# Up projection of an encoder block: products gathered in two PSUM banks, the convolution summed in PSUM, and every engine's order written by hand

## The chip, the cores and the metric

One core of one Trainium2 chip. The metric is the device time of one execution in microseconds (us), lower is better. The kernel computes in float32 throughout.

## The reference

One layer of an encoder on 1024 tokens of width 1024: a norm, an input projection, a pooling mixer beside differential attention, an output projection with residual, then the part that matters here, the gated MLP (`D_FF` is 2816, so `w_up` is 1024 x 5632):

```python
h = rmsnorm(x, norm_ffn_g[l])
u = causal_dwconv(h @ w_up[l], conv_w[l], conv_b[l])      # out[t] = b + sum_j w[j] * u[t-2+j], per channel
gate, val = jnp.split(u, 2, axis=-1)
x = x + (jax.nn.silu(gate) * val) @ w_down[l]
return rmsnorm(x, norm_final_g)
```

## The kernel before, in words

**Products.** Float32 values are split into a rounded high part and a low rest (`split`, lines 83 to 91: ScalarE casts the high part on line 86, VectorE or GpSimd subtracts for the low part on line 87). One product of 128x128 weights with 512 columns is three matmuls (`mm3`, lines 78 to 81: high x high, high x low, low x high).

**Up projection.** The 5632 columns are taken as 22 blocks `f` (NF), each with 128 gate and 128 value channels. A block is a 2x2 by 2x2 block product: gate and value against the two halves of the contraction (weights a11, a12, a21, a22, each 128x512), and the two halves of the contraction against the two halves of the tokens (H = 512). It is done with seven products in place of eight: the sums S1 to S4 of the weights (GpSimd, lines 731 to 734) stand against sums T1 to T4 of the tokens' blocks, which `norm2b` makes once (lines 635 to 660). `product` (line 706) is 4 x 3 = 12 matmuls into one PSUM tile of 512 columns. So a block has 84 matmuls. Results, channels on the partitions and 1024 tokens along the free axis: `ug` (gate) and `uv` (value).

`up` (lines 739 to 782) issues per block P1 (operand B11), P6 (T2), P2 (B21), P5 (T1), P7 (T3), P4 (T4), P3 (B22). The sums of products are made by VectorE out of PSUM: on line 726 `ug` left = P2 + s1 (s1 is ScalarE's copy of P1, line 720), on line 748 u2 = P6 + s1, on line 758 u3 = P7 + u2, on line 759 u2 += P5, on line 760 `uv` right = P5 + u3, on line 765 `uv` left = u3 - P4, on line 767 `ug` right = P3 + u2. P6 and P7 lie in one PSUM tile of two banks, P5 and P3 in another (tag S, two tiles in all); P1, P2 and P4 take tiles of one bank (tag B, four).

**Convolution and gate.** For value and gate: ScalarE makes o = u * w + bias (line 773), VectorE adds two shifted taps (line 775, `scalar_tensor_tensor` of 1023 and 1022 columns, all of it in SBUF), ScalarE applies Silu to the gate (line 778), and GpSimd multiplies the two (line 780). `store` (lines 789 to 810) writes the result to DRAM as the operand of the down projection and makes sums of it on VectorE (line 797, or lines 803 to 805 for every second block).

**Ahead.** P1 and P2 of the first four blocks (AHEAD, lines 812 to 819) are computed while the last token blocks are normalized.

**What sets the order.** Outside of regions marked otherwise, the framework's scheduler orders each engine's instructions by a model of time and their place in the program. From line 825 on, where the down projection begins, the DMA queue (SP) is issued in program order. Down again has seven products, P1 to P7 of 11 x 4 x 3 matmuls (`load`, `unit`, lines 876 to 905), whose operands are read back, split and used three steps ahead.

**Buffers.** `raw` (4) holds loaded weights, `Q` (6) the sums S, `hi` and `lo` (5 each) split weights, `T` (5) s1, u2, u3, `K` (4) ug and uv, `E` (6) the tiles of the convolution.

Of the kernel before, what the change touches and what calls it, by code (L numbers as in the profile page):

```python
# [14 lines left out]
AF = mybir.ActivationFunctionType  # L15
# [4 lines left out]
T = 1024  # L20
# [30 lines left out]
def block_kernel(ctx, tc, x, xT, pos, wv, wqk, wp, wo, wup, wdn, cols, invf, rcnt, gffn, gfin,  # L51
# [25 lines left out]

    def mm3(dst, lhi, llo, rhi, rlo, first, last):
        mm(dst, lhi, rhi, start=first, stop=False)  # L79
        mm(dst, lhi, rlo, start=False, stop=False)  # L80
        mm(dst, llo, rhi, start=False, stop=last)  # L81

    def split(src, hi, lo, scale=None, eng=None):

# [550 lines left out]
    def norm2b(tt):  # L635
# [65 lines left out]

    acts, opd, ugs, s1s = {}, {}, {}, {}

    def product(dst, w, nm):
        hi, lo = opnd[nm]
        for kt in range(4):
            c = slice(kt * P, (kt + 1) * P)
            j, k = divmod(kt, 4 // len(hi))  # L710
            mm3(dst, w[0][:, c], w[1][:, c], hi[j][:, k, :], lo[j][:, k, :], kt == 0, kt == 3)

    add, sub = ALU.add, ALU.subtract
    tens = nc.vector.tensor_tensor

    def up_p1(f, w):
        p1 = psB(f"P1{f}")
        product(p1, w, "B11")
        s1s[f] = st("T", f"s1{f}")
        nc.scalar.copy(out=s1s[f], in_=p1)  # L720

    def up_p2(f, w):
        p2 = psB(f"P2{f}")
        product(p2, w, "B21")
        ugs[f] = st("K", f"ug{f}")
        tens(out=ugs[f][:, 0:H], in0=p2, in1=s1s[f], op=add)

    def up_prep(f, ahead):
        a11, a12, a21, a22 = [wraw(f, a, pc, "b" if ahead and a == 0 else "") for a in range(2) for pc in range(2)]
        S1, S2, S3, S4 = [st("Q", f"S{i}{f}") for i in range(4)]  # L730
        nc.gpsimd.tensor_tensor(out=S1, in0=a21, in1=a22, op=add)  # L731
        nc.gpsimd.tensor_tensor(out=S2, in0=S1, in1=a11, op=sub)  # L732
        nc.gpsimd.tensor_tensor(out=S3, in0=a11, in1=a21, op=sub)  # L733
        nc.gpsimd.tensor_tensor(out=S4, in0=a12, in1=S2, op=sub)  # L734
        return a11, a12, a22, S1, S2, S3, S4

    waiting = []

    def up(f, ahead, prep, then):
        a11, a12, a22, S1, S2, S3, S4 = prep  # L740
        if not ahead:
            up_p1(f, wsplit(a11, f"a11{f}"))
        s1 = s1s[f]
        p67 = psS(f"P67{f}")
        p6, p7 = p67[:, 0:H], p67[:, H:T]
        product(p6, wsplit(S2, f"S2{f}"), "T2")
        u2 = st("T", f"u2{f}")
        tens(out=u2, in0=p6, in1=s1, op=add)
        if not ahead:
            up_p2(f, wsplit(a12, f"a12{f}"))  # L750
        ug = ugs[f]
        uv = st("E" if f == order[0] else "K", f"uv{f}")
        p53 = psS(f"P53{f}")
        p5, p3 = p53[:, 0:H], p53[:, H:T]
        product(p5, wsplit(S1, f"S1{f}"), "T1")
        product(p7, wsplit(S3, f"S3{f}", nc.gpsimd), "T3")
        u3 = st("T", f"u3{f}")
        tens(out=u3, in0=p7, in1=u2, op=add)
        tens(out=u2, in0=p5, in1=u2, op=add)
        tens(out=uv[:, H:T], in0=p5, in1=u3, op=add)  # L760
        if waiting:
            store(*waiting.pop())
        p4 = psB(f"P4{f}")
        product(p4, wsplit(a22, f"a22{f}"), "T4")
        tens(out=uv[:, 0:H], in0=u3, in1=p4, op=sub)  # L765
        product(p3, wsplit(S4, f"S4{f}"), "B22")
        tens(out=ug[:, H:T], in0=p3, in1=u2, op=add)  # L767
        prep = then()
        acc = []
        for a, u in ((1, uv), (0, ug)):  # L770
            cc = 16 + (a * NF + f) * 4
            o = st("E", f"ac{f}{a}")
            nc.scalar.activation(o, u, AF.Identity, bias=col[:, cc + 3:cc + 4], scale=col[:, cc + 2:cc + 3])  # L773
            for d in (1, 2):
                nc.vector.scalar_tensor_tensor(out=o[:, d:T], in0=u[:, 0:T - d], scalar=col[:, cc + 2 - d:cc + 3 - d],  # L775
                                               in1=o[:, d:T], op0=ALU.mult, op1=ALU.add)
            if a == 0:
                nc.scalar.activation(o, o, AF.Silu)  # L778
            acc.append(o)
        nc.gpsimd.tensor_tensor(out=acc[1], in0=acc[1], in1=acc[0], op=ALU.mult)  # L780
        waiting.append((f, acc[1]))
        return prep
# [313 lines left out]
```

## Time and profile before

| | |
|---|---|
| median of 3 runs | 1082.02 us (1080.84 to 1086.27) |
| the profiled execution | 1083.04 us, of which the span of instructions is 1081.3 us |
| matmuls (PE) busy | 1022.4 us, 95% of the span |
| VectorE (DVE) busy | 883.2 us, 82% |
| ScalarE (ACT) busy | 484.1 us, 45% |
| GpSimd (POOL) busy | 417.6 us, 39% |
| mean granted TensorE clock | 0.991 of full speed |

The span runs from the first to the last instruction; the profiled execution's own time is 1.7 us longer. In rows of instructions the columns are start (us from the span's start), duration (us), engine, line of the kernel, operation, tile written <- tiles read, shapes, and in brackets how long the engine had been idle before it and what ended that. Matmuls overlap in the pipeline: a row of 0.39 us is followed by the next after 0.23 us, so the distance between starts is what one matmul costs. Tile names are cut by the profile: `P<-T,S16h` is a product of the up projection with the high part of S1 of block 6, `dP` one of the down projection.

### The profile page before, as it was taken

The page shows a single profiled execution, that of the slowest core. Times are in us where ns is not written, and L with a number is a line of the kernel's source. Part 1 is how long each engine was busy: PE and PEld are TensorE (multiplying, and loading weights), DVE is VectorE, ACT ScalarE, POOL GpSimd, SP SyncE. Part 2 cuts the span into 40 slices and gives each one's busy share as a digit, 9 for nine tenths or more (in the row PEclk, how much of TensorE's full clock was granted, in tenths as well). Part 3 has the DMA queues.
Part 4 walks back from the last instruction along what each step waited for, and adds up shares of the span by engine and source line. Part 5 has one row for each costly group of instructions (what it writes and reads, how often), then busy time and mean ns, then how long its engine had stood idle before and what let it go on. Part 6 is the DMA issues. An engine that isn't in the chain of part 4 may idle for free.

```text
span 1081.3 us, 13516 instructions
## 1 busy us (share of the span) xinstructions
PE 1022.4 (95%) x4612; PEld 834.9 (77%) x4612; DVE 883.2 (82%) x1195; ACT 484.1 (45%) x842; POOL 417.6 (39%) x306
## 2 busy tenths in 40 slices
PE   8999999998998998989999999999999899999995
PEld 6888888886886876767777778778778688877884
DVE  6465887989757496999988998898998976699895
ACT  6822554556546263333433333333334554334533
POOL 0000122221221066565465465465465100586462
PEclk9999999999999999999999999999999999999999
DMA  8627543323335222232222222222222885442215
GB/s 305 226 96 266 173 147 108 102 97 116 126 117 166 78 88 69 88 117 78 98 98 99 97 98 105 89 102 106 86 108 96 322 312 203 157 144 100 98 57 187
DMA packets 67972, 143.88 MB, mean 133 GB/s; under 512 B 8512, under 2 KB 9664, under 8 KB 67904
## 3 DMA queue, kind: packets, MB, share of 16 engines
q1 hardware_dynamic: 67904, 143.03, 37.7%
q8 instruction: 36, 0.59, 0.2%
q14 instruction: 32, 0.26, 0.1%
HBM read 105.78 MB, written 37.22 MB: 132 GB/s over the span
## 4 chain that ended last, share of the span: by engine, by line
PE 39%; DVE 16%; issue 14%; POOL 13%; DMA 3%; ACT 2%; POOLq 0%; SPq 0%; DVEq 0%; ACTq 0%
PE dP L80 5%; PE dP L81 5%; PE dP L79 5%; DVE ac L775 4%; POOL ac L780 3%; PE po L81 3%; PE po L79 2%; PE po L80 2%; PE sc L386 2%; POOL S L732 2%; PE O L433 2%; POOL S L734 2%; DMA wu<-in_wup 2%; POOL S L731 2%; PE P L79 2%
## 5 line engine op out<-in xcount | busy, mean ns | idle before, releaser
L403 POOL TENSOR_SCALAR e<-e,sm 128x128 f32<-128x128 f32 (+7 forms) x32 | 29.9, 936 | 175.6 <-DMA k<-tsk 69.5
L775 DVE SCALAR_TENSOR_TENSOR ac<-uv,col,ac 128x1023 f32<-128x1023 f32 (+1 forms) x44 | 78.2, 1777 | 6.3 <-ACT ac L773 5.7
L775 DVE SCALAR_TENSOR_TENSOR ac<-ug,col,ac 128x1023 f32<-128x1023 f32 (+1 forms) x44 | 76.6, 1741 | 0.8 <-ACT ac L773 0.7
L780 POOL TENSOR_TENSOR ac<-ac,ac 128x1024 f32<-128x1024 f32 x22 | 60.3, 2740 | 37.9 <-ACT ac L778 37.8
L731 POOL TENSOR_TENSOR S<-wu,wu 128x512 f32<-128x512 f32 x22 | 30.2, 1374 | 107.2 <-DMA wu<-in_wup 107.1
L773 ACT ACTIVATE ac<-uv,col 128x1024 f32<-128x1024 f32 x22 | 27.4, 1245 | 89.7 <-DVE uv L765 89.7
L399 ACT ACTIVATE e<-sc,mx 128x128 f32<-128x128 f32 (+7 forms) x64 | 47.2, 743 | 32.3 <-DVE mx L389 16.8
L773 ACT ACTIVATE ac<-ug,col 128x1024 f32<-128x1024 f32 x22 | 27.4, 1245 | 52.3 <-DVE ug L767 52.3
L386 PE MATMUL sc<-K,Q 128*128 128x512 f32 (+3 forms) x192 | 42.6, 351 | 0.7 <-ACT e L399 0.7
L853 POOL TENSOR_TENSOR T<-B22w,B12w 128x512 f32<-128x512 f32 x11 | 17.5, 1595 | 65.0 <-DMA arP<-S 63.3
L733 POOL TENSOR_TENSOR S<-wu,wu 128x512 f32<-128x512 f32 x18 | 37.4, 2079 | 0.0
L386 PEld LDWEIGHTS sc<-K,Q 128*128 128x128 f32 x192 | 32.4, 189 | 6.0 <-ACT e L399 1.2
L564 DVE TENSOR_TENSOR X<-X,po 128x512 f32<-128x512 f32 x32 | 21.6, 681 | 16.3 <-PE po L81 16.2
L421 ACT COPY at<-tp 128x512 f32<-128x512 f32 (+3 forms) x48 | 21.6, 484 | 28.8 <-PE tp L417 28.8
L778 ACT ACTIVATE ac<-ac 128x1024 f32<-128x1024 f32 x22 | 23.3, 1061 | 25.0 <-DVE ac L775 25.0
L433 PE MATMUL O<-at,V 128*128 128x256 f32 (+1 forms) x160 | 34.0, 358 | 0.0
L433 PEld LDWEIGHTS O<-at,V 128*128 128x128 f32 x160 | 29.8, 190 | 4.0
L389 DVE TENSOR_REDUCE mx<-sc 128x1 f32<-128x640 f32 (+3 forms) x32 | 32.2, 1014 | 0.4
L734 POOL TENSOR_TENSOR S<-wu,S 128x512 f32<-128x512 f32 x18 | 32.5, 1804 | 0.0
L732 POOL TENSOR_TENSOR S<-S,wu 128x512 f32<-128x512 f32 x18 | 31.3, 1738 | 1.4
L87 DVE TENSOR_TENSOR wP<-B12w,wP 128x512 fp32r<-128x512 f32 x30 | 26.4, 903 | 3.2 <-ACT wP L86 1.8
L404 DVE SCALAR_TENSOR_TENSOR e<-e,sm,e 128x640 f32<-128x640 f32 (+3 forms) x16 | 17.4, 1090 | 10.3 <-POOL e L403 10.3
(2488 smaller groups left out, 3645.4 us busy)
## 6 DMA issues: line engine op xcount, KB each, us to landing
wu<-in_wup SPq DMA_DIRECT2D x88, 256.0 KB, 2.6
S<-s SPq DMA_DIRECT2D x22, 512.0 KB, 3.2
arP<-S SPq DMA_DIRECT2D x44, 256.0 KB, 2.6
arP<-A SPq DMA_DIRECT2D x33, 256.0 KB, 4.3
Q<-q SPq DMA_DIRECT2D x64, 128.0 KB, 2.9
A<-ac SPq DMA_DIRECT2D x11, 512.0 KB, 2.9
xs<-in_x SPq DMA_DIRECT2D x8, 512.0 KB, 7.5
K<-k SPq DMA_DIRECT2D x8, 512.0 KB, 4.8
```

What stands on the lines that cost most here:

```text
L79: mm(dst, lhi, rhi, start=first, stop=False)
L80: mm(dst, lhi, rlo, start=False, stop=False)
L81: mm(dst, llo, rhi, start=False, stop=last)
L386: mm(sc[:, k0:k1], qst[h, grp][n * 2 + hl][:, qc], kst[h][n][:, k0:k1], start=hl == 0, stop=hl == 1)
L399: nc.scalar.activation(ee[n], scs[n][:, 0:L], AF.Exp, bias=nmx[:, n:n + 1], accum_out=sums[:, n:n + 1])
L433: mm(O[:, c0:256], V[j][:, h * P:(h + 1) * P], at[:, j, c0:256], start=j == 0, stop=j == nj - 1)
L731: nc.gpsimd.tensor_tensor(out=S1, in0=a21, in1=a22, op=add)
L732: nc.gpsimd.tensor_tensor(out=S2, in0=S1, in1=a11, op=sub)
L734: nc.gpsimd.tensor_tensor(out=S4, in0=a12, in1=S2, op=sub)
L773: nc.scalar.activation(o, u, AF.Identity, bias=col[:, cc + 3:cc + 4], scale=col[:, cc + 2:cc + 3])
L775: nc.vector.scalar_tensor_tensor(out=o[:, d:T], in0=u[:, 0:T - d], scalar=col[:, cc + 2 - d:cc + 3 - d], in1=o[:, d:T], op0=ALU.mult, op1= ...
L780: nc.gpsimd.tensor_tensor(out=acc[1], in0=acc[1], in1=acc[0], op=ALU.mult)
```

## The change

Only the up projection and its convolution are touched, and the place where they begin.

- P1, P6, P7 and P4 are added up by TensorE in one bank X, P5 and P3 in another, Z. ScalarE copies X out after each product but the first of them is s1: s1 after P1, u2 after P6, u3 after P7, `uv` left after P4. T4 changes its sign for this. VectorE keeps three sums: `ug` left = P2 + s1, `uv` right = Z + u3 (read between P5 and P3), `ug` right = Z + u2. The four ahead blocks keep separate banks for P6, P7, P4 and have VectorE add (five sums).
- ScalarE writes the convolution's o into PSUM (two-bank tiles, tag S), and VectorE's taps read and write it there. The gate's product moves from GpSimd to VectorE (`after4`).
- Weights are loaded two blocks ahead (`h`), a22 into a tile of tag Q; sums S are made one block ahead (`g`); the convolution of a block (`p`) runs beside the products of the next one.
- In the loop over blocks the order of all five queues is the order of the program. One block issues P6, P5, P7, P1 of the next, P4, P3, P2 of the next.

```diff
-    def mm3(dst, lhi, llo, rhi, rlo, first, last):
+    def mm3(dst, lhi, llo, rhi, rlo, first, last, more=False):
...
-        nc.gpsimd.tensor_tensor(out=t4, in0=t2, in1=t4, op=sub)
+        nc.gpsimd.tensor_tensor(out=t4, in0=t4, in1=t2, op=sub)
...
+    def conv(u, a, src):
+        cc = 16 + (a * NF + u.f) * 4
+        o = psS(f"o{a}{u.f}")
+        nc.scalar.activation(o, src, AF.Identity, bias=col[:, cc + 3:cc + 4], scale=col[:, cc + 2:cc + 3])
+        return o
+    def tap(u, a, d, src, o):
+        cc = 16 + (a * NF + u.f) * 4
+        nc.vector.scalar_tensor_tensor(out=o[:, d:T], in0=src[:, 0:T - d], scalar=col[:, cc + 2 - d:cc + 3 - d],
+                                       in1=o[:, d:T], op0=ALU.mult, op1=ALU.add)
...
+    def after0(p):
+        tap(p, 1, 1, p.uv, p.o1)
+        p.o0 = conv(p, 0, p.ug)
+    def after1(p):
+        tap(p, 1, 2, p.uv, p.o1)
+    def after2(p):
+        tap(p, 0, 1, p.ug, p.o0)
+    def after3(p):
+        tap(p, 0, 2, p.ug, p.o0)
+    def after4(p):
+        g = st("E", f"g{p.f}")
+        nc.scalar.activation(g, p.o0, AF.Silu)
+        p.act = st("E", f"ac{p.f}")
+        tens(out=p.act, in0=p.o1, in1=g, op=ALU.mult)
+    def up(p, u, g, h):
+        new = g is not None and not g.ahead
+        if u.ahead:
+            x6 = psB(f"P6{u.f}")
+        else:
+            x6 = u.X
+        product(x6, u.S2w, "T2", u.ahead)
+        up_split(u, "S3", nc.gpsimd)
+        if p:
+            after0(p)
+        if not u.ahead:
+            c11(u, u.Y)
+        if u.ahead:
+            u2 = u.s1
+            tens(out=u2, in0=x6, in1=u.s1, op=add)
+        else:
+            u2 = st("T", f"u2{u.f}")
+            nc.scalar.copy(out=u2, in_=x6)
+        z = psB(f"Z{u.f}")
+        product(z, u.S1w, "T1")
+        if new:
+            up_split(g, "a11")
+        if p:
+            after1(p)
+        if h:
+            up_load(h, "a21")
+        x7 = psB(f"P7{u.f}") if u.ahead else x6
+        product(x7, u.S3w, "T3", u.ahead)
+        up_split(u, "a22")
+        if p:
+            after2(p)
...
+            nc.scalar.copy(out=u3, in_=x7)
+        if new:
+            g.X = psB(f"P1{g.f}")
+            product(g.X, g.a11w, "B11")
+        up_split(u, "S4")
+        if p:
+            after3(p)
+        if g:
+            up_sum(g, 1)
+            up_sum(g, 3)
...
+        x4 = psB(f"P4{u.f}") if u.ahead else x6
+        product(x4, u.a22w, "T4", u.ahead)
+        u.uv = st("E" if u.n < 2 else "K", f"uv{u.f}")
+        tens(out=u.uv[:, H:T], in0=z, in1=u3, op=add)
+        if new:
+            g.s1 = st("T", f"s1{g.f}")
+            nc.scalar.copy(out=g.s1, in_=g.X)
+            up_split(g, "a12")
+        if p:
+            after4(p)
+        if g:
+            up_sum(g, 2)
...
+        product(z, u.S4w, "B22", False)
...
+            nc.scalar.copy(out=u.uv[:, 0:H], in_=x4)
+        if g:
+            up_split(g, "S2")
+        u.o1 = conv(u, 1, u.uv)
+        if p:
+            store_a(p)
+        if g:
+            up_sum(g, 4)
...
+        if new:
+            g.Y = psB(f"P2{g.f}")
+            product(g.Y, g.a12w, "B21")
+        if g:
+            up_split(g, "S1")
+        tens(out=u.ug[:, H:T], in0=z, in1=u2, op=add)
+        if p:
+            store_b(p)
...
+            up_load(u, "a21", "a22", "a11", "a12")
+            for k in (1, 3, 2, 4):
+                up_sum(u, k)
...
+    with tc.manual_schedule(engines={E.PE, E.Activation, E.DVE, E.Pool, E.SP}):
+        for n in range(NF):
+            up(us[n - 1] if n else None, us[n], us[n + 1] if n + 1 < NF else None, us[n + 2] if n + 2 < NF else None)
+        p = us[-1]
+        for fn in (after0, after1, after2, after3, after4, store_a, store_b):
+            fn(p)
```

`up_split` is the split of a weight tile (cast on ScalarE, rest on VectorE, for S3 on GpSimd), `up_sum` one of the sums S on GpSimd, `up_load` a load on SP, `c11` the sum on `ug`'s left half, `store_a` and `store_b` the two halves of the former `store`.

## Rows read from the trace of the kernel before

**Rows 1.** The page, parts 1 and 2: TensorE and VectorE busy, granted clock in 40 slices.

```profile
PE 1022.4 (95%) x4612; PEld 834.9 (77%) x4612; DVE 883.2 (82%) x1195; ACT 484.1 (45%) x842; POOL 417.6 (39%) x306
...
PEclk9999999999999999999999999999999999999999
```

**Rows 2.** Stretches, up's products only: stretch, length, PE busy (matmuls), clock, DMA share, GB/s.

```profile
388.30:418.50 30.20, 24.81 (x96) 0.94 0.26 88
418.50:517.95 99.45, 88.59 (x362) 0.97 0.27 98
517.95:820.24 302.29, 290.17 (x1260) 1.00 0.26 96
820.24:854.43 34.19, 30.23 (x130) 1.00 0.55 189
```

**Rows 3.** Timeline of TensorE: first and last of 22 matmuls without a wait.

```profile
843.56 0.39 PE L79 MATMUL P<-T,S321h 128*128 128x512 f32 x1
...
848.32 0.39 PE L81 MATMUL P<-T,a2221l 128*128 128x512 f32 x1
```

**Rows 4.** Waits of TensorE: who waited <- for whom: us in total, times, longest.

```profile
PE P L79 <- DVE ug L767: 15.7, 19, 1.7
...
PE P L79 <- DVE u L758: 4.6, 4, 3.2
```

**Rows 5.** Timeline, all engines, block 6: what stands before one of these waits.

```profile
654.47 0.39 PE L81 MATMUL P<-T,S26l 128*128 128x512 f32 x1
...
656.06 2.21 DVE L775 SCALAR_TENSOR_TENSOR ac<-uv,col,ac 128x1022 f32<-128x1022 f32 x1
...
658.19 0.68 DVE L767 TENSOR_TENSOR ug<-P,u 128x512 f32<-128x512 f32 x1
...
658.92 0.50 PE L79 MATMUL P<-T,S16h 128*128 128x512 f32 x1 [0.44 <-DVE ug L767]
```

**Rows 6.** The steady stretch: all engines, then VectorE's line 87 and its line 775.

```profile
517.95:820.24 302.29, 290.17 (x1260) 235.34 (x1260) 275.59 (x285) 115.95 (x166) 168.96 (x90) 1.00 0.26 96
...
517.95:820.24 302.29, 95.72 (x91) 1.00 0.26 96
...
517.95:820.24 302.29, 107.22 (x60) 1.00 0.26 96
```

**Rows 7.** VectorE by line: durations in ns, least/median/longest; out of PSUM, SBUF alone, into PSUM.

```profile
L759 DVE TENSOR_TENSOR u<-P,u x22: 676/678/680, 435.6 to 850.2; 128x512 f32<-128x512 f32 x22
...
L775 DVE SCALAR_TENSOR_TENSOR ac<-uv,col,ac x44: 1269/1490/2410, 439.9 to 857.0; 128x1023 f32<-128x1023 f32 x22, 128x1022 f32<-128x1022 f32 x22
...
L388 DVE MEMSET sc<- x32: 112/112/112, 124.4 to 306.0; 64x64 f32 x32
...
L392 DVE MEMSET sc<- x16: 165/165/165, 108.6 to 241.1; 64x128 f32 x16
```

**Rows 8.** ScalarE: the copy out of PSUM, the convolution's start, a cast.

```profile
L720 ACT COPY s<-P x22: 576/577/598, 399.0 to 836.2; 128x512 f32<-128x512 f32 x22
...
L773 ACT ACTIVATE ac<-uv,col x22: 1242/1245/1248, 437.5 to 853.3; 128x1024 f32<-128x1024 f32 x22
...
417.85 0.62 ACT L86 CAST S20h<-S 128x512 fp32r<-128x512 f32 x1 [0.50 <-POOL S L732]
```

**Rows 9.** GpSimd: the sum S2 of block 0, and the gate's product (line 780).

```profile
416.09 1.73 POOL L732 TENSOR_TENSOR S<-S,wu000b 128x512 f32<-128x512 f32 x1
...
L780 POOL TENSOR_TENSOR ac<-ac,ac x22: 2395/2842/2862, 454.6 to 864.3; 128x1024 f32<-128x1024 f32 x22
```

**Rows 10.** From TensorE to VectorE: a product's last matmul, and the reader that had waited.

```profile
438.90 0.39 PE L81 MATMUL P<-T,S211l 128*128 128x512 f32 x1
...
439.33 0.69 DVE L748 TENSOR_TENSOR u<-P,s 128x512 f32<-128x512 f32 x1 [1.84 <-PE P L81]
```

**Rows 11.** Timelines at the end of up: VectorE, and SP's last store of an activation.

```profile
844.16 0.68 DVE L87 TENSOR_TENSOR aP10l<-arP,aP10h 128x512 fp32r<-128x512 f32 x1
...
868.74 0.38 SPq L786 DMA_DIRECT2D A<-ac  x1
```

More of the change, by code (lines that the diff above doesn't have):

```diff
@@ L699, in block_kernel, with product @@
             norm2b(tt - 1)
-    acts, opd, ugs, s1s = {}, {}, {}, {}
-    def product(dst, w, nm):
+    acts, opd, U = {}, {}, {}
+    def product(dst, w, nm, first=True):
         hi, lo = opnd[nm]
@@ L710, in product @@
             j, k = divmod(kt, 4 // len(hi))
-            mm3(dst, w[0][:, c], w[1][:, c], hi[j][:, k, :], lo[j][:, k, :], kt == 0, kt == 3)
+            mm3(dst, w[0][:, c], w[1][:, c], hi[j][:, k, :], lo[j][:, k, :], first and kt == 0, kt == 3, not first)
     add, sub = ALU.add, ALU.subtract
     tens = nc.vector.tensor_tensor
[L716 to L782, printed above, removed]
@@ new lines, in block_kernel, with __init__, up_load, up_sum @@
+    pool = nc.gpsimd.tensor_tensor
+    class Up:
+        def __init__(u, n):
+            u.n, u.f, u.ahead = n, order[n], n < AHEAD
+    def up_load(u, *which):
+        for nm in which:
+            a, pc = {"a11": (0, 0), "a12": (0, 1), "a21": (1, 0), "a22": (1, 1)}[nm]
+            r = st("Q" if nm == "a22" else "raw", f"w{nm}{u.f}")
+            nc.sync.dma_start(out=r, in_=wup[u.f, a, :, pc * 4:pc * 4 + 4, :].rearrange("p a b -> p (a b)"))
+            setattr(u, nm, r)
+    def up_sum(u, k):
+        t = st("Q", f"S{k}{u.f}")
+        setattr(u, f"S{k}", t)
+        x, y, op = {1: ("a21", "a22", add), 2: ("S1", "a11", sub), 3: ("a11", "a21", sub), 4: ("a12", "S2", sub)}[k]
+        pool(out=t, in0=getattr(u, x), in1=getattr(u, y), op=op)
@@ L787, in dram, with store_a @@
         return t
-    def store(f, a):
-        i = f % NG
-        if f < NG:
+    def store_a(u):
+        i, a = u.f % NG, u.act
+        if u.f < NG:
             acts[i] = a
@@ L796, in store @@
             s34 = acts["s34"] = st("E", f"s34{i}")
-            nc.vector.tensor_tensor(out=s34[:, 0:H], in0=a[:, 0:H], in1=a[:, H:T], op=sub)
+            tens(out=s34[:, 0:H], in0=a[:, 0:H], in1=a[:, H:T], op=sub)
             return
@@ new lines, in up @@
+    def up(p, u, g, h):
[29 more added lines that the diff above has]
+            after2(p)
+        u3 = st("T", f"u3{u.f}")
+        if u.ahead:
+            tens(out=u3, in0=x7, in1=u2, op=add)
+        else:
+            nc.scalar.copy(out=u3, in_=x7)
[8 more added lines that the diff above has]
+            up_sum(g, 3)
+        if h:
+            up_load(h, "a22")
+        x4 = psB(f"P4{u.f}") if u.ahead else x6
[10 more added lines that the diff above has]
+            up_sum(g, 2)
+        if h:
+            up_load(h, "a11")
+        product(z, u.S4w, "B22", False)
+        if u.ahead:
+            tens(out=u.uv[:, 0:H], in0=u3, in1=x4, op=add)
+        else:
+            nc.scalar.copy(out=u.uv[:, 0:H], in_=x4)
[6 more added lines that the diff above has]
+            up_sum(g, 4)
+        if h:
+            up_load(h, "a12")
+        if new:
[6 more added lines that the diff above has]
+            store_b(p)
@@ L816, in block_kernel @@
+    us = [Up(n) for n in range(NF)]
+    for u in us[:AHEAD]:
+        x = psB(f"P1{u.f}")
+        product(x, ahead_w.pop(0), "B11")
+        u.s1 = st("T", f"s1{u.f}")
+        nc.scalar.copy(out=u.s1, in_=x)
+        y = psB(f"P2{u.f}")
+        product(y, ahead_w.pop(0), "B21")
+        c11(u, y)
+        if u.n == 0:
             norm2b(7)
-            first = up_prep(0, True)
+            up_load(u, "a21", "a22", "a11", "a12")
+            for k in (1, 3, 2, 4):
+                up_sum(u, k)
@@ L818, in block_kernel @@
             for tt in range(4, 8):
                 osplit("B22", tt, fb["B22", tt], nc.gpsimd if tt % 2 else None)
-    for n, f in enumerate(order):
-        first = up(f, n < AHEAD, first, lambda: up_prep(order[n + 1], n + 1 < AHEAD) if n + 1 < NF else None)
-    store(*waiting.pop())
+    up_split(us[0], "S2")
+    up_split(us[0], "S1")
+    up_load(us[1], "a21", "a22", "a11", "a12")
+    E = mybir.EngineType
+    with tc.manual_schedule(engines={E.PE, E.Activation, E.DVE, E.Pool, E.SP}):
[4 more added lines that the diff above has]
+            fn(p)
```

29 lines of the change are left out of this document (17 added, 12 removed).

## The prediction, made blind

> **What bounds the kernel now.** I read the page first: TensorE is busy 95% of the span, VectorE 82%, and the granted clock is at or near the upper level, 2.4 GHz, in all 40 slices [rows 1]. As rows of matmuls overlap, "95%" hides small gaps, so I then counted the up projection's matmuls in stretches [rows 2] and set against them what one costs without a wait: 22 in a row start 4.76 us apart from first to last, 4.76/21 = 0.2267 us each [rows 3]. A product is 12 of them, 2.72 us; a block 84, 19.04 us. Excess over that, by stretch:
>
> - 388.3 to 418.5 (the products ahead): 30.2 - 96 x 0.2267 = 8.4 us, some of it transposes of the norm.
> - 418.5 to 517.95 (the four ahead blocks and the way into the next): 99.45 - 362 x 0.2267 = 17.4 us.
> - 517.95 to 820.24 (15 steady blocks): 302.29 - 285.6 = 16.7 us, 1.11 per block; a block takes 20.15 us.
> - 820.24 to 854.43 (last block, into down): 34.19 - 29.5 = 4.7 us.
>
> After the first stretch that is 38.8 us, the most that this change can win. The waits of TensorE name the cause: 19 waits for line 767, `ug` right [rows 4]. One of them: P3 of block 6 issues its last matmul at 654.47, but VectorE is in the taps until 658.19 and only then reads the bank, which P5 of the next block needs; TensorE resumes at 658.92 [rows 5]. The bound of a steady block is VectorE being late, not the matmuls: it is busy 275.6 of 302.3 us [rows 6].
>
> **The change, engine by engine, per steady block.** TensorE: the same 84 matmuls, 19.04 us. The loads are as many as before (256 KB each) and DMA has room (share 0.26) [rows 2]; nothing for them. SP waits in order now: a load stands behind the store of `act`, but loads are two blocks ahead, 38 us, so that order hides.
>
> VectorE before: seven sums out of PSUM, six low parts, four taps, two sums of `store` on average; busy 275.6/15 = 18.4 us. Low parts cost 95.72/91 = 1.05 us, taps 107.22/60 = 1.79 us [rows 6]. A sum with a PSUM operand always takes 0.68, while a tap in SBUF takes 1.27 to 2.41 [rows 7]; what lengthens it is there only where both operands are in SBUF. After: three sums 2.04, six low parts 6.3, `store` 1.4, the gate's product about one tap, and four taps with o in PSUM. No row shows an instruction that reads and writes PSUM at once. Bounds: 1.27 us (the least tap; nothing suggests cheaper) to 2.54 (twice that, if reading and writing one bank took turns). The nearest rows: reading PSUM costs what SBUF does, and writing it costs (165 - 112)/64 = 0.83 ns per element [rows 7]. So I take 1.27; VectorE's sum is 2.04 + 6.3 + 1.4 + 5 x 1.27 = 16.1 us, under 19.04.
>
> ScalarE: 115.95/15 = 7.7 us [rows 6]; three more copies at 0.58 make 9.5 us, and writing o into PSUM is not shown; I leave it at 1.245 [rows 8] (twice that would be 2.5 more: 12 us, still no bound; less would free nothing that is waited for). GpSimd: 168.96/15 = 11.3 us [rows 6] less the gate's product, 2.84 [rows 9]: 8.4.
>
> Order decides the rest. In block time P6 ends at 2.72, P5 at 5.44, P7 at 8.16, P1 of the next at 10.88, P4 at 13.60, P3 at 16.32, P2 of the next at 19.04. A reader starts 0.43 us after the start of a product's last matmul [rows 10], so 0.2 after the next product's start. Three checks:
>
> - Handoffs in bank X: end of product, 0.2, copy 0.58, next product into X. About 0.85 us against the 2.72 of the other product between them. Queued on ScalarE behind such a copy are one or two casts of 0.6; before it, at most a cast and a convolution, 1.9 us. Covered.
> - Handoff in bank Z: VectorE must read P5 (with u3) before P3 at 13.60. Its order: `c11` 0.9; a11's low part waits for the cast behind u2's copy, 2.72 + 0.2 + 0.58 + 0.6 = 4.1, ends 5.2; tap 6.4; a22 7.4; tap 8.7; S4's low part waits for the cast behind u3's copy, 9.6, ends 10.6; tap 11.9; the sum 12.6. One us to spare.
> - S2 and S1 of the next block end at about 16 and 18, wanted at 19.0 and 21.8.
>
> So TensorE should run through. I leave 0.2 us per block for contention on low parts, of 1.11: 15 x 0.91 = 13.7 us won (bounds 0 to 16.7).
>
> **The early blocks.** An ahead block has five products, 13.6 us, and five sums on VectorE. There P3 is due at 10.88 and VectorE reads Z at 12.6: 1.7 us late in two blocks, 3.4. Block 0 has no taps, but its S2 is third, not second, on GpSimd: 1.7 [rows 9]. Of 17.4 us some 5.4 stay: 12.0 won (bounds 5 to 15). The first stretch stays as it is; the scheduler may shift it by 2 us either way.
>
> **The end.** In the last block no P1 stands between P7 and P4, so TensorE waits 0.85 for u3's copy and another 0.9 for Z, and it starts down afterwards. VectorE then owes four taps, the gate and the stores, some 8.4 us, besides down's low parts. In the trace before, down's splits stand among these already (844.16) and a store of up's result is issued at 868.74, far into down [rows 11]: instructions outside of a region mix with it. Of 4.7 us I take nothing back (bounds -10 to +3).
>
> Sum: 13.7 + 12.0 + 0 = 25.7 us off the profiled execution's own 1083.0: **1057 us**, when all else stays. That execution lies 1.0 us above the median of 1082.0.
>
> **A rule against it.** In the steady block P1, P6, P7 and P4 share one bank and each starts only when ScalarE has copied; by the rows, a handoff is 0.85 us under a cover of 2.72 [rows 8, 10]. The Trainium skill (Perfetto Trace Analysis, Optimizing Tensor Performance, Matmuls) says that independent groups should rotate through banks so that the evacuation of one overlaps the next group. By that rule the handoffs would show and the sum would be that of the rival on them below. No run so far shows a shared bank, so the trace neither agrees nor differs.
>
> **Rivals.**
>
> - Half the gain, 1070 us. VectorE's fixed order meets GpSimd at the wrong time: the taps take their former 1.79 us (the read of Z then ends at 5.2 + 3 x 1.79 + 2 x 1.05 + 0.6 = 13.3, still in time), the low parts more than their mean besides. At 1.5 us for each of the three it is 4.1 + 3 x 1.5 + 3 x 1.79 + 0.6 = 14.6, 1.0 late; in most of 18 blocks, 0.7 on average, 12.6 us are lost: 1057 + 13. For it: VectorE's order can no longer bend. Against: the taps left the SBUF that they contended for.
> - The tail is bare, 1068 us. Down's loads and splits stand behind the last block's ordered tail: 0.2 + sum 0.7 + convolution 1.2 + two taps 2.5 + Silu 1.1 + gate 1.3 + stores 2.1 + two low parts 1.4, 10.5 us of TensorE. For it: the queues are ordered to the end. Against: rows 11.
> - Taps in PSUM cost 2.3 to 2.54 us. At 2.3 the read of Z ends at 5.2 + 3 x 2.3 + 2 x 1.05 + 0.6 = 14.8, 1.2 late in 18 blocks, 22 us: 1079, no change. At 2.54 VectorE's own sum is 16.1 + 4 x 1.27 = 21.2 us against a block of 20.15 now: 1.05 x 18 = 19 us more, less the 12 of the early blocks, 1090, slower. Against: neither reading nor writing PSUM costs extra in the rows.
> - Handoffs in bank X are not covered: slower, 1117 us. Place: ScalarE's one ordered queue, where a copy stands behind a convolution or Silu that waits for VectorE. Price: three copies at 0.85 and Z's read at 0.93, 3.5 us per block, over 18 blocks 63 us on top of the forecast less its own 15 x 0.2, 1054. It decides from (1083 - 1054)/18 = 1.6 us per block. For it: the one bank, and that Silu waits for the last tap. Against: the cover of 2.72. The rule of the Trainium skill above is about this mechanism.
> - The change does what it says and the time doesn't move: TensorE catches up but down starts no earlier, as its weights' tiles are still held. 1080. Against: the operand B11 is last read by the P1 that the last block but one issues, 8.2 + 13.6 = 22 us before up's end, and down's loads can start there.
>
> **How the numbers follow.** Forecast 0.55, half the gain 0.17, bare tail 0.10, taps dear 0.09 (half no change, half slower), handoffs 0.05, nothing 0.04. What a measurement of this kernel can tell from no change is about 0.5%, 5.4 us: faster is below 1076.6. Faster: 0.55 + 0.17 + 0.10 = 0.82 and 0.01 of the last rival, 0.83; same: half of the dear taps and the rest of the last, 0.08; slower: the other half and the handoffs, 0.09. Low end: all of the steady 16.7, 15 of the early, 3 of the end: 1083 - 35 = 1048. High end: half the gain and the bare tail together, 1057 + 13 + 11 = 1081; it leaves out the dear taps' upper half, the handoffs and little else.
>
> **What would show it.** Right: TensorE's starts in the middle of up stay 0.2267 us apart over whole blocks (19.0 to 19.3 us per block), line 767's waits are gone, taps are 1.27 us, VectorE is busy 16 us per block, and up ends near 828. Wrong: taps above 1.8 us; waits of TensorE for ScalarE's copies (bank X) or for VectorE's sum of Z; a gap over 3 us where down begins; a clock at 1.2 GHz in stretches where it is full now.

## The result and the profile after

The kernel after takes 1055.69 us, the median of 4 runs (1052.37 to 1056.45), beside 1083.42 (1080.84 to 1086.27) for the kernel before: ratio 0.9738, 95% interval [0.9703, 0.9772]. The forecast was 1057 us in a range of 1048 to 1081. The profiled execution took 1052.37 us, its span 1050.6.

First the page's busy times; they answer to [rows 1]:

```profile
PE 1012.6 (96%) x4612; PEld 836.3 (80%) x4612; DVE 782.6 (74%) x1141; ACT 510.1 (49%) x896; POOL 324.9 (31%) x284
```

VectorE has 101 us less to do, GpSimd 93 less, ScalarE 26 more. The same four stretches as [rows 2], cut at the same numbers of matmuls of the up projection (stretch, length, PE busy and matmuls, clock, DMA share, GB/s; all of TensorE's matmuls are counted here, in [rows 2] up's alone):

```profile
385.61:418.31 32.70, 25.86 (x112) 0.95 0.28 97
418.31:505.28 86.97, 85.01 (x363) 0.98 0.31 106
505.28:790.88 285.60, 285.60 (x1262) 1.00 0.30 104
790.88:821.54 30.66, 29.98 (x132) 1.00 0.41 139
```

The third is the steady stage: 1260 matmuls in 285.60 us, without one gap. That is 1260 x 0.2267, and each block takes 19.04 us. All engines in it, then VectorE's line 87 (low parts) and its line 753 (the taps), for [rows 6]:

```profile
505.28:790.88 285.60, 285.60 (x1262) 236.57 (x1260) 207.48 (x240) 138.79 (x211) 103.27 (x76) 1.00 0.30 104
...
505.28:790.88 285.60, 62.25 (x90) 1.00 0.30 104
...
505.28:790.88 285.60, 76.80 (x60) 1.00 0.30 104
```

TensorE's waits (who waited <- for whom: us in total, times, longest). What stands above 15 us in [rows 4] has gone, and nothing in the steady blocks has come in its place:

```profile
PE dP L80 <- DVE wP L87: 5.0, 5, 1.9
PE P L79 <- ACT S20h L86: 3.5, 1, 3.5
...
PE Z L79 <- DVE uv L864: 1.1, 2, 0.5
PE P L81 <- DVE S21l L87: 0.7, 1, 0.7
```

**Where the time went.** The table cuts every kernel of this study at the same counts of matmuls: the 96 of the products ahead, the next 362 (ahead blocks and the way in), 1260 steady ones, the last 130, and from the start of the last one to the end of the span. Times in us. The stretch ahead of the up projection, where the instructions are the same, is left out.

| kernel | ahead products | early blocks | steady | last block | down | sum |
|---|---|---|---|---|---|---|
| before | 30.2 | 99.4 | 302.3 | 34.0 | 227.1 | 692.9 |
| after | 32.7 | 87.0 | 285.6 | 30.7 | 229.1 | 665.0 |
| e1_taps_sbuf | 32.7 | 90.3 | 285.6 | 30.7 | 229.9 | 669.1 |
| e2_old_conv | 32.6 | 95.9 | 286.2 | 30.7 | 229.6 | 675.0 |
| e3_no_order | 32.9 | 83.9 | 285.6 | 30.6 | 226.3 | 659.2 |
| e4_vector_sums | 33.0 | 87.5 | 285.6 | 32.9 | 227.5 | 666.4 |
| e5_no_cover | 32.6 | 89.5 | 300.2 | 32.1 | 226.5 | 680.8 |
| e6_load_before_z | 33.2 | 97.3 | 304.8 | 38.7 | 226.7 | 700.6 |
| e7_load_elsewhere | 33.0 | 92.6 | 285.6 | 30.7 | 229.1 | 671.0 |
| e9_ends | 31.2 | 86.6 | 285.6 | 29.7 | 227.2 | 660.2 |
| g1_three_undone | 32.6 | 88.7 | 288.2 | 30.6 | 226.2 | 666.3 |
| g2_two_buffers | 30.0 | 97.9 | 302.6 | 38.5 | 223.8 | 692.7 |
| g3_before_z | 30.8 | 101.7 | 300.4 | 33.9 | 226.7 | 693.5 |
| g4_no_order_ends | 30.0 | 85.1 | 285.6 | 31.5 | 226.1 | 658.2 |

From before to after: +2.5, -12.5, -16.7, -3.3, +2.0, together -28.0; the medians differ by 27.7. Each row is one profiled execution.

### The profile page after: what moved, and what is told of

The parts are those of the page before. It is cut to its first block, busy times and chain, and to the rows that moved or that the text cites. A ratio compares the mean times of both kernels' runs of the same rounds, so it can differ in the third digit from the quotient of the medians.

```text
span 1050.6 us, 13509 instructions
## 1 busy us (share of the span) xinstructions
PE 1012.6 (96%) x4612; PEld 836.3 (80%) x4612; DVE 782.6 (74%) x1141; ACT 510.1 (49%) x896; POOL 324.9 (31%) x284
## 4 chain that ended last, share of the span: by engine, by line
PE 70%; DVE 7%; POOL 3%; issue 3%; ACT 2%; DMA 1%; SPq 0%; POOLq 0%; DVEq 0%; ACTq 0%
PE P L81 9%; PE P L79 9%; PE P L80 9%; PE dP L80 4%; PE dP L81 4%; PE dP L79 4%; PE Z L79 4%; PE Z L80 4%; PE Z L81 4%; PE po L81 3%; PE po L79 3%; PE sc L386 2%; PE po L80 2%; PE O L433 2%; PE pp L79 1%
## 5 line engine op out<-in xcount | busy, mean ns | idle before, releaser
L403 POOL TENSOR_SCALAR e<-e,sm 128x128 f32<-128x128 f32 (+7 forms) x32 | 29.7, 932 | 174.9 <-DMA k<-tsk 68.9
L735 POOL TENSOR_TENSOR S<-wa,wa 128x512 f32<-128x512 f32 x44 | 64.7, 1490 | 0.9 <-DMA wa<-in_wup 0.9
L399 ACT ACTIVATE e<-sc,mx 128x128 f32<-128x128 f32 (+7 forms) x64 | 47.1, 741 | 32.5 <-DVE mx L389 16.7
L753 DVE SCALAR_TENSOR_TENSOR o<-ug,col,o 128x1023 f32<-128x1023 f32 (+1 forms) x44 | 56.3, 1281 | 0.0
L753 DVE SCALAR_TENSOR_TENSOR o<-uv,col,o 128x1023 f32<-128x1023 f32 (+1 forms) x44 | 56.3, 1279 | 0.0
L735 POOL TENSOR_TENSOR S<-S,wa 128x512 f32<-128x512 f32 x22 | 28.3, 1287 | 73.8 <-DVE a224l L87 4.8
L735 POOL TENSOR_TENSOR S<-wa,S 128x512 f32<-128x512 f32 x22 | 28.5, 1294 | 51.0 <-issue 50.9
L848 ACT COPY u<-P 128x512 f32<-128x512 f32 x18 | 10.6, 587 | 69.2 <-PE P L81 69.2
L386 PEld LDWEIGHTS sc<-K,Q 128*128 128x128 f32 x192 | 32.7, 190 | 5.7 <-ACT e L399 0.9
L748 ACT ACTIVATE o<-ug,col 128x1024 f32<-128x1024 f32 x22 | 26.6, 1210 | 20.1 <-DVE ug L896 20.1
L828 ACT COPY u<-P 128x512 f32<-128x512 f32 x18 | 10.6, 587 | 50.0 <-PE P L81 50.0
L564 DVE TENSOR_TENSOR X<-X,po 128x512 f32<-128x512 f32 x32 | 21.7, 682 | 14.7 <-PE po L81 14.6
L806 DVE TENSOR_TENSOR ac<-o,g 128x1024 f32<-128x1024 f32 x22 | 26.9, 1224 | 7.1 <-ACT g L804 6.9
L748 ACT ACTIVATE o<-uv,col 128x1024 f32<-128x1024 f32 x22 | 26.7, 1214 | 9.6 <-DVE uv L878 9.6
L867 ACT COPY s<-P 128x512 f32<-128x512 f32 x18 | 10.6, 587 | 33.1 <-PE P L81 33.1
```

The lines of the kernel that those rows point to most:

```text
L386: mm(sc[:, k0:k1], qst[h, grp][n * 2 + hl][:, qc], kst[h][n][:, k0:k1], start=hl == 0, stop=hl == 1)
L399: nc.scalar.activation(ee[n], scs[n][:, 0:L], AF.Exp, bias=nmx[:, n:n + 1], accum_out=sums[:, n:n + 1])
L403: nc.gpsimd.tensor_scalar(out=e1, in0=e1, scalar1=sums[:, 3:4], scalar2=1.0, op0=ALU.mult, op1=ALU.mult)
L735: pool(out=t, in0=getattr(u, x), in1=getattr(u, y), op=op)
L748: nc.scalar.activation(o, src, AF.Identity, bias=col[:, cc + 3:cc + 4], scale=col[:, cc + 2:cc + 3])
L753: nc.vector.scalar_tensor_tensor(out=o[:, d:T], in0=src[:, 0:T - d], scalar=col[:, cc + 2 - d:cc + 3 - d], in1=o[:, d:T], op0=ALU.mult, op ...
```

## The experiments

The question is which part of the change brings the 16.7 us of the steady blocks, and what its other parts cost or bring. The e-runs and g1 and g4 edit the kernel after, g2 and g3 the kernel before. Ratios are to the kernel before, run on the same chip.

### e1_taps_sbuf: the convolution's sums back in SBUF

```diff
-        o = psS(f"o{a}{u.f}")
+        o = st("E", f"o{a}{u.f}")
...
-        g = st("E", f"g{p.f}")
-        nc.scalar.activation(g, p.o0, AF.Silu)
-        p.act = st("E", f"ac{p.f}")
-        tens(out=p.act, in0=p.o1, in1=g, op=ALU.mult)
+        nc.scalar.activation(p.o0, p.o0, AF.Silu)
+        p.act = p.o1
+        tens(out=p.act, in0=p.o1, in1=p.o0, op=ALU.mult)
```

> One part undone: o and the taps in SBUF again, Silu and the gate's product in place; the order and TensorE's sums stay. My theory (a steady block is bound by TensorE as long as VectorE reads Z before P3): the taps cost 1.28 to 1.79 us again, the read of Z ends between 12.0 and 13.3 us of the block against 13.6, so at most 0.3 us per block are lost: 1056 to 1061 us. Rival (it was the taps' contention with GpSimd in SBUF that made TensorE wait): 1.1 us per block are lost again in 18 blocks, about 1076 us.

1058.95 us, 0.9757 [0.974, 0.9774]. The steady stage stays at 285.6; 3.3 us are lost in the early blocks. The taps of the value, VectorE's line 753 (least/median/longest in ns), in this kernel:

```profile
L753 DVE SCALAR_TENSOR_TENSOR o<-uv,col,o x44: 1265/1463/2307, 434.6 to 829.4; 128x1023 f32<-128x1023 f32 x22, 128x1022 f32<-128x1022 f32 x22
```

and in the kernel after, with o in PSUM:

```profile
L753 DVE SCALAR_TENSOR_TENSOR o<-uv,col,o x44: 1274/1280/1286, 435.0 to 826.5; 128x1023 f32<-128x1023 f32 x22, 128x1022 f32<-128x1022 f32 x22
...
L748 ACT ACTIVATE o<-uv,col x22: 1209/1215/1217, 432.0 to 820.8; 128x1024 f32<-128x1024 f32 x22
...
L806 DVE TENSOR_TENSOR ac<-o,g x22: 1219/1224/1225, 447.1 to 834.9; 128x1024 f32<-128x1024 f32 x22
```

So PSUM takes the spread out of the taps, as forecast, but the steady blocks didn't need it.

### e2_old_conv: and the gate's product back on GpSimd

e1 with `pool(...)` in place of `tens(...)` for the product.

> The whole convolution as before (o in SBUF, gate's product on GpSimd), order and TensorE's sums stay. VectorE loses the product (1.2 us per block), GpSimd gains 2.4 to 2.8 us (about 9.5 per block) and overlaps more with low parts and taps. My theory: the read of Z is in time or some tenths late, 1056 to 1066 us. Rival (contention): 1076 us or more.

1066.08 us, 0.9826 [0.9811, 0.9842], the upper end of what I had expected. Again no steady loss to speak of (286.2); the early blocks lose 8.9 us, where TensorE now waits for casts of S2 (3.0 and 1.8 us in two blocks). The new convolution pays in the early blocks alone.

### e3_no_order: the written order taken away

```diff
-    with tc.manual_schedule(engines={E.PE, E.Activation, E.DVE, E.Pool, E.SP}):
+    if True:
```

> The hand-written order undone: the same instructions, the loads two blocks ahead and the buffers stay, but the scheduler orders all queues in the loop over blocks. If what VectorE has to do is the cause (13.9 us per block now, 18.4 before), the scheduler's order loses little: 1056 to 1062 us. Rival (the order is what keeps the reads of the banks in time): a wait of about 1 us per block comes back, 1070 to 1083 us.

1050.44 us, 0.968 [0.9664, 0.9696]: **faster than the change itself**, and outside of what I or the rival expected. Its interval lies below that of the change. With the same program, the scheduler's own order wins 3.1 us in the early blocks and 2.8 where down begins, and leaves the steady blocks as they are.

### e4_vector_sums: P6, P7, P4 in banks of their own, added by VectorE

```diff
-        if u.ahead:
-            x6 = psB(f"P6{u.f}")
-        else:
-            x6 = u.X
-        product(x6, u.S2w, "T2", u.ahead)
+        x6 = psB(f"P6{u.f}")
+        product(x6, u.S2w, "T2", True)
...
-            nc.scalar.copy(out=u2, in_=x6)
+        tens(out=u2, in0=x6, in1=u.s1, op=add)
```

and the same for P7 and P4: every block is made as the ahead blocks are.

> The sums in PSUM undone in part: P6, P7 and P4 have banks of their own in every block and VectorE adds them as in the ahead blocks (six sums per block, three copies less on ScalarE); P5 and P3 still share Z, order and convolution stay. VectorE's load goes to 13.9 + 3 x 0.6 = 15.7 us of 19.04. My theory: u3's sum starts at 8.4, S4's low part follows at 9.1, a tap, and the read of Z ends at 11.6 to 12.4, before 13.6: same time, 1055 to 1060 us. Rival (TensorE's sums are what took VectorE off the path): 0.5 us or more per block, 1065 us or more.

1057.54 us, 0.9744 [0.9727, 0.976]. Steady 285.6 with VectorE at 197.38 us in 240 (15.7 per block). Bank X, the first words of the change, isn't what brings the gain either.

### e5_no_cover: the handoff in bank X laid bare

P7 is issued straight behind P6, and P5 after it, in the 18 blocks with bank X; the same matmuls in another order.

```diff
+        if not u.ahead:
+            product(x6, u.S3w, "T3", False)
         z = psB(f"Z{u.f}")
         product(z, u.S1w, "T1")
...
-        product(x7, u.S3w, "T3", u.ahead)
+        if u.ahead:
+            product(x7, u.S3w, "T3", True)
```

> In the 18 blocks that add up in bank X, TensorE issues P7 straight behind P6, and P5 after it: no product in another bank covers this handoff. My theory (handoff 0.85 us by the rows): 18 x 0.85 = 15 us more, 1071 us, all of it in waits for u2's copy. Rival, the copy stands behind other work on ScalarE: 1.6 us or more per block, 1085 us or more. Rival, a bank can be handed over at no cost: 1056 us.

1073.22 us, 0.9899 [0.987, 0.9928]. TensorE's waits name the place:

```profile
PE P L79 <- ACT u L828: 12.2, 18, 0.7
```

One uncovered handoff costs (300.2 - 285.6)/15 = 0.97 us per block; the forecast had worked out 0.85. With the cover it costs nothing: no wait for a copy of bank X stands in the steady blocks of the kernel after.

### e6_load_before_z and e7_load_elsewhere: the same work, in two places

Both give VectorE two taps more per block, which add the same products again: the output is another, and only the time is of use. In e6 they stand just ahead of the read of Z; in e7 they stand earlier, ahead of S4's low part, where VectorE pauses for 1.76 us in the kernel after.

```diff
     def after3(p):
         tap(p, 0, 2, p.ug, p.o0)
+        tap(p, 0, 2, p.ug, p.o0)
+        tap(p, 0, 2, p.ug, p.o0)
```

```diff
     def after1(p):
         tap(p, 1, 2, p.uv, p.o1)
+        tap(p, 1, 2, p.uv, p.o1)
     def after2(p):
         tap(p, 0, 1, p.ug, p.o0)
+        tap(p, 0, 1, p.ug, p.o0)
```

> The last tap of the gate is done three times (the output adds it three times): 2.4 us more for VectorE per block, right in front of the read of Z. VectorE's load is then 16.3 of 19.04 us. My theory (the place in the order counts): the read ends at 12.0 + 2.4 = 14.4 against 13.6, so P3 is 0.8 us late in 18 blocks, 14 us, and 2.4 late in two or three ahead blocks, 6 us: about 1076 us. Rival (only VectorE's load against the block counts): 1056 us.

> The same 2.4 us more per block for VectorE, as one repetition of the value's second tap and one of the gate's first tap (the output adds both twice): in front of the pause of 1.8 us in which VectorE waits for S4's high part. My theory: the pause takes it up but for about 0.6 us, the read of Z ends at 12.6 at most: 1055 to 1060 us. Rival (load): the same time as with the last tap done three times.

e6: 1090.27 us, 1.0059 [1.0038, 1.0081], 0.6% slower than the kernel before. e7: 1061.35 us, 0.979 [0.9762, 0.9817], 1.35 above my range; what it loses against the change lies in the early blocks (92.6 us against 87.0). TensorE's wait and the busy times in 240 steady microseconds of e6:

```profile
PE Z L79 <- DVE uv L866: 28.0, 21, 3.2
```

```profile
540.00:780.00 240.00, 227.86 (x993) 185.05 (x992) 193.60 (x215) 109.77 (x168) 79.39 (x59) 1.00 0.28 97
```

and the same stretch of e7:

```profile
540.00:780.00 240.00, 240.00 (x1061) 198.79 (x1060) 205.76 (x229) 119.39 (x178) 87.06 (x65) 1.00 0.30 104
```

VectorE is busier in e7 (205.76 against 193.60) and TensorE never stops; in e6 it loses (304.8 - 285.6)/15 = 1.28 us per block. So VectorE's load is not what counts here, but whether the read of Z ends before P3 is due. In e6 that read ends 14.6 us into the block, 1.0 after P3's time, and P3 starts 0.14 later. My size for e6 was too small: the steady blocks lost 1.28 us each, not 0.8, and its early and last blocks lost 18 us more, of which I had counted about 8.

### g1_three_undone: e2, e3 and e4 at once

The edits of e2, e3 and e4 together.

> The former convolution (o in SBUF, gate product on GpSimd), VectorE's sums of P6, P7 and P4 in banks of their own, and the scheduler's order in place of the written one, all three undone together; what stays of the change is that P5 and P3 add up in a one-bank tile Z and that weights are loaded two blocks ahead and sums S made one block ahead. My theory: the steady gain does not need any of the three, because what cost the time was the tile that line 767 freed too late; steady blocks stay at 19.04 to 19.15 us (stage of 1260 matmuls 285.6 to 287.5 us), the loss is in the early blocks as in the run with the old convolution (some 95 us against 87), in all 1060 to 1068 us. Rival: the three stand in for one another, each alone was not needed because the other two kept VectorE in time; together VectorE is back at some 18 us per block, steady blocks at 19.7 us or more (stage over 295 us), 1072 to 1083 us.

1056.06 us, 0.9746 [0.9725, 0.9767]. What gave the change its name is undone, the convolution, the hand-written order and the sums in bank X, and the time is that of the change. That is below my 1060 to 1068: the early blocks took 88.7 us, not 95. All engines in the steady stage:

```profile
511.54:799.74 288.20, 287.65 (x1261) 236.03 (x1260) 287.68 (x270) 120.19 (x166) 166.38 (x91) 1.00 0.28 101
```

VectorE is busy for 287.68 of 288.20 us, 19.2 per block, more than the 18.4 of the kernel before, and TensorE for 287.65. VectorE has one sum less per block than before (270 instructions against 285), but they are stretched: a low part takes 123.04/90 = 1.37 us, against 1.05. The three are not substitutes for one another: without all of them 2.6 us come back of 16.7. And it was not VectorE's busy time that cost the kernel before its time. The reason that I gave for it in advance, the tile that line 767 frees, is what g2 tests.

### g2_two_buffers and g3_before_z: one part alone, in the kernel before

g2 gives P5 and P3 of alternating blocks a tile each, so that what line 767 frees is wanted a block later:

```diff
-        p67 = psS(f"P67{f}")
-        p6, p7 = p67[:, 0:H], p67[:, H:T]
+        p6, p7 = psB(f"P6{f}"), psB(f"P7{f}")
```

g3 adds up P5 and P3 in one bank, which saves VectorE line 759 (`product` takes a further argument `first`, as in the change):

```diff
-        p5, p3 = p53[:, 0:H], p53[:, H:T]
+        p5 = p3 = p53[:, 0:H]
...
-        tens(out=u2, in0=p5, in1=u2, op=add)
...
-        product(p3, wsplit(S4, f"S4{f}"), "B22")
+        product(p3, wsplit(S4, f"S4{f}"), "B22", False)
```

> The kernel before with one edit: P6 and P7 take one-bank tiles of tag B, so that the two two-bank tiles of tag S are left to P5 and P3 of alternating blocks. All of VectorE's work stays (18.4 us per block). My theory: the tile that line 767 frees is then wanted a whole block later, the 15.7 us of waits for line 767 go, and with them most of the steady excess; steady stage 286 to 292 us (before 302.3), 1066 to 1074 us. Rival: VectorE's load and order are the bound; another of its sums is late instead (u3, uv or the reads of P1 to P4 that free tag B), steady stage over 297 us, 1077 to 1084 us.

> The kernel before with one edit: P5 and P3 add up in one bank, and VectorE's sum u2 += P5 (line 759, 0.68 us per block) is left out; the tile is still of tag S and still freed by line 767. My theory: line 767 still stands behind the taps, so its waits stay (10 us or more in all) and only a little is won from VectorE's 0.68 us; steady stage 298 to 302 us, 1075 to 1083 us. Rival: adding up in one bank is itself what brings the steady gain, by one sum less ahead of line 767; steady stage under 292 us, 1073 us or less.

g2: 1082.71 us, 0.9995 [0.9979, 1.0011]. My theory of line 767's tile falls. Its waits are gone, and nearly as many have come for another of VectorE's sums, line 759 there, `uv` right:

```profile
PE P L79 <- DVE uv L759: 13.0, 15, 2.4
```

g3: 1084.0 us, 1.0002 [0.998, 1.0025], 1 us above my range: line 767 (766 there) is waited for still, as I expected.

```profile
PE P L79 <- DVE ug L766: 11.8, 18, 1.2
```

Both leave VectorE less busy (252.55 and 240.46 us in some 302 and 300, against 275.59 before) and win nothing. The wait of [rows 4] names who came last, not who is the cause.

**What is left.** All kernels with steady blocks of 19.04 to 19.2 us, and e5 and e6 beside what was put into them, load weights two blocks ahead, a block before the sums S are made of them, and emit a block's convolution and stores among the next block's products. The kernel before, g2 and g3 load and sum in one step, a block ahead (`up_prep`), and emit the convolution in its own block. GpSimd's waits in the kernel before:

```profile
POOL S L731 <- DMA wu<-in_wup: 107.1, 21, 6.7
```

and VectorE's:

```profile
DVE s L803 <- POOL ac L780: 8.8, 8, 1.1
DVE s L797 <- POOL ac L780: 8.7, 8, 1.1
```

GpSimd stands and waits for weights in 21 blocks, 5.1 us each; its sums and the gate's product behind them are late, and in 16 blocks VectorE stops 1.1 us at the `store` that reads this product. In g2 (72.5 us between 520 and 790) and g3 (70.3) GpSimd waits for loads as it did before (79.3); in the kernel after and in all its variants there is no such wait in that stretch.

The trace of the kernel before shows that these waits are stations of a loop in which TensorE has no part. One turn, from the chain of work that ended last (start, us, what; `ac L775` are the taps):

```profile
658.87 0.61 DVE a226l L87
659.49 2.52 DMA wu<-in_wup
...
662.15 1.28 POOL S L731
...
669.07 2.82 POOL ac L780
...
671.91 0.69 DVE s L803
...
675.14 2.31 DVE ac L775
...
678.68 0.69 DVE ug L767
679.36 0.61 DVE a2217l L87
```

The first load for the next block starts 0.03 us after VectorE has finished the low part of a22, in all 15 steady blocks; GpSimd's four sums stand behind this load, the gate's product behind the sums, VectorE's `store` behind the product, and behind that, in VectorE's queue, `uv` left, the taps (with ScalarE's o ahead of them), line 767 and the next low part of a22. From one such low part to the next it is 19.78 to 20.50 us, where TensorE's matmuls need 19.04. The same steps follow each other in g2 and g3, which take out a wait or a sum but leave the load and the convolution where they were. So line 767 is one station of this loop, and TensorE waits for whichever of the delayed sums frees its next bank.

The change touches this loop in two places, with the earlier loads and with the convolution a block later. A kernel before with one of them alone wasn't tried, nor one with the new order of products alone (P1 and P2 issued a block ahead). Which of these is needed for the 16.7 us isn't shown; Z alone is not enough (g3).

### e9_ends and g4_no_order_ends: the ends mended

e9 lets block 0 begin with P5, whose S1 GpSimd makes first, makes the sums in the order 1, 2, 3, 4, and gives P4 of the last block its own bank.

```diff
+        if u.n == 0:
+            z = psB(f"Z{u.f}")
+            product(z, u.S1w, "T1")
...
+        if not g:
+            up_split(u, "S4")
...
+        apart = u.ahead or not g
+        x4 = psB(f"P4{u.f}") if apart else x6
...
-            for k in (1, 3, 2, 4):
+            for k in (1, 2, 3, 4):
```

> A version for the two ends: block 0 starts with P5, which needs only S1, and makes S2 second of the sums; in the last block P4 has a bank of its own and S4 is split ahead of u3's copy. My theory: the 3.5 us idle in front of P6 of block 0 goes, and with it most of the 8 matmuls at the lower clock (1.9 us), and 1.4 us in the last block: 5 to 7 us less than the changed kernel, 1049 to 1051 us. Rival: down starts no earlier, as its splits are late: 1054 us.

1050.17 us, 0.9681 [0.966, 0.9702], in the range, but not by the parts that I had named: 1.5 us less in the products ahead and 0.4 in the early blocks, where I had counted on over 5; 1.0 in the last block; and 1.9 in down, where I had counted on nothing. g4 takes the written order away as well (e3's line):

> The change without the written order of the queues (the scheduler orders them), and with the edits at the ends (block 0 starts with P5, its sums S are made in the order 1, 2, 3, 4; in the last block P4 has its own bank and S4 is split earlier). Each of the two was some 5 to 6 us faster than the change. My theory: they win partly in the same places (both have down at 226 to 227 us against 229), so together 1045 to 1050 us, steady blocks at 19.04. Rival: the scheduler's own order had won at the same ends already, no more than either alone: 1050 to 1052 us.

1048.21 us, 0.9671 [0.9653, 0.9689], the fastest here. Its stages sum up to 658.2 against 659.2 and 660.2 of e3 and e9: the two win mostly in the same places. Its time lies in my range, but by the intervals g4 can't be told from e3 or e9.

## Why the prediction was right, point by point

- **The sum.** By stages it came to 28.0 us, forecast 25.7: 3.0 more in the steady blocks and 0.5 in the early ones, 1.3 more at the end, and 2.5 less in the products ahead. That the total is this near is in part luck.
- **The price of TensorE** was right to the digit: 0.2267 us per matmul, 19.04 per block.
- **The steady blocks**: won 16.7, forecast 13.7. The mis-sized term is the 0.2 us per block left "for contention on low parts". VectorE takes 207.48/15 = 13.8 us per block, not 16.1: a low part costs 62.25/90 = 0.69 us, where I kept the 1.05 of before, and 6 x 0.36 is 2.2 of the 2.3. Taps (76.80/60 = 1.28; I took 1.27), ScalarE (138.79/15 = 9.25; 9.5) and GpSimd (6.9; 8.4) came out near.
- **The handoff in Z.** I had the read end at 12.6 us of the block, P3 due at 13.60. The timeline of block 6, P6's first matmul, the read and P3's first:

```profile
635.38 0.39 PE L79 MATMUL P<-T,S26h 128*128 128x512 f32 x1
...
646.68 0.68 DVE L864 TENSOR_TENSOR uv<-Z,u 128x512 f32<-128x512 f32 x1
...
648.98 0.39 PE L79 MATMUL Z<-B,S46h 128*128 128x512 f32 x1
```

  It ends at 11.98, and e6 showed what 1.0 us past the due time costs: the whole gain.
- **The handoffs in X and the rule against them.** The copies are covered in the kernel after, and e5 lays one bare at 0.97 us (forecast 0.85). The Trainium skill (Perfetto Trace Analysis, Optimizing Tensor Performance, Matmuls) wants independent groups in rotating banks. The trace agrees: without a product between, the handoff shows (e5, 0.97 us); where a product of 2.72 us in another bank stands between, the copy runs under it and no wait is left. So the kernel after does what the rule wants, with banks in turn, and the rule was not against it.
- **The early blocks**: won 12.5, forecast 12.0. The parts were off in ways that cancel. I had P3 1.7 late in two blocks: block 11 loses 0.82 in all (14.42 us, not 13.60), block 1 loses 1.84, of which 0.7 is a wait for S2. S2 as third of GpSimd's sums cost more than 1.7, and in the stretch ahead, which I had left as it was: +2.5. The wait, the slow matmuls behind it and the clock of block 0 in the timeline and the stretches of the kernel after:

```profile
418.31 0.80 PE L79 MATMUL P<-T,S20h 128*128 128x512 f32 x1 [3.53 <-ACT S20h L86]
418.90 0.63 PE L80 MATMUL P<-T,S20h 128*128 128x512 f32 x1
```

```profile
418.31:422.20 3.89, 3.86 (x10) 0.58 0.69 221
...
418.31:433.78 15.47, 15.44 (x61) 0.90 0.35 120
433.78:448.20 14.42, 13.87 (x61) 1.00 0.11 36
448.20:463.64 15.44, 14.18 (x62) 1.00 0.28 97
```

  After 3.53 us of standing still the granted clock is 0.58 in the first 3.9 us, most of them at the lower level, 1.2 GHz, and 0.90 in the whole block. The first nine matmuls take 3.88 us in place of 2.04: 1.8 us for which I had counted nothing, although the trace of the kernel before has eight such matmuls, from 434.68 on, behind waits of 3.08 and 0.93 us.
- **The end**: forecast 0, measured -3.3 in the last block and +2.0 in down. The two delays are there, 0.84 us for u3's copy (forecast 0.85), and P3 0.59 late (0.9). Down's instructions mix with the ordered tail, as [rows 11] had suggested: here a cast and two matmuls of down stand ahead of P3. Down's own waits for low parts come to 5.0 us in the list of waits above (4.5 in the kernel before).

```profile
815.74 0.50 PE L79 MATMUL P<-T,a2221h 128*128 128x512 f32 x1 [0.68 <-ACT u L848]
...
818.19 0.62 ACT L86 CAST wP<-B11w 128x512 fp32r<-128x512 f32 x1
818.60 0.62 PE L79 MATMUL dP<-wP,aP10h 128*128 128x512 f32 x2
...
819.05 0.39 PE L79 MATMUL Z<-B,S421h 128*128 128x512 f32 x1
```

- **The step that failed is the diagnosis.** I wrote that the bound of a steady block is VectorE being late at line 767 and credited the gain to its shorter list of work. The lateness was there and its sum was right, since all of the excess went. But g1 keeps TensorE running with VectorE busier than before, and g2 removes that wait and wins nothing. I had seen loads "two blocks ahead" only as what hides SP's order, and priced them at nothing; what separates the fast kernels from the slow ones is that, and the order in the program, the two places where the change touches the loop shown above; which of them counts stays open. I also misread a line of [rows 5]: the matmul of 654.47 belongs to P6 of block 6 (its tile is S26l). P3 of block 16, the one before it, issues its last here:

```profile
654.24 0.39 PE L81 MATMUL P<-B,S416l 128*128 128x512 f32 x1
```

  VectorE reads that bank at 658.19, so that it was late holds.
- **"Order decides the rest"** was right for the place of single reads (e6 against e7). That it must be written by hand was not: e3 is 5.8 us faster without, by the stages.

## What to carry to other kernels

A wait that TensorE shows names the last one in a loop of engines; before costing a change by it, follow the loop back, here to the engine that waits for a load, and test the named tile alone, which is two lines of edit. A handoff in one bank cost 0.97 us bare here and nothing under another product of 2.72, so try products in between before spending banks. Where a program already emits work a block ahead, try the scheduler's order before writing one by hand: here the hand-written one lost 5.8 us at its ends.

## What the runs showed of the hardware

Where an operand of VectorE lies sets what GpSimd beside it costs. The same sum S2 of the block that follows block 6, beside the same tap, with o in PSUM (the kernel after):

```profile
641.84 1.28 DVE L753 SCALAR_TENSOR_TENSOR o<-ug,col,o 128x1023 f32<-128x1023 f32 x1
642.07 1.29 POOL L735 TENSOR_TENSOR S<-S,wa 128x512 f32<-128x512 f32 x1 [4.77 <-DVE a226l L87]
```

and with o in SBUF (e1):

```profile
644.73 1.28 DVE L753 SCALAR_TENSOR_TENSOR o<-ug,col,o 128x1023 f32<-128x1023 f32 x1
644.96 2.20 POOL L735 TENSOR_TENSOR S<-S,wa 128x512 f32<-128x512 f32 x1 [3.80 <-DVE a226l L87]
```

Here GpSimd pays 0.9 us; in e1's value taps VectorE pays, up to 2.31 against 1.27. The Trainium skill (GPSIMD Engine Reference, Specifications) says that GpSimd's interfaces to SBUF are shared with VectorE and contend with VectorE's instructions of two SBUF inputs; these rows agree. I had expected a cheaper tap, not that the sums beside it would shrink as well. An instruction that reads and writes the same PSUM tile cost nothing extra (1.28 us, against 1.27 at the least in SBUF), and ScalarE's 1024 columns take 1.21 us into PSUM, 1.245 into SBUF [rows 8].
